# The two split instructions of each weight chunk, scheduled ahead of other ScalarE and VectorE work

## The chip, the core and the metric

The kernel runs on one core of a Trainium2 chip. The core has a matrix engine (TensorE, PE in the profile), three engines for elementwise work (VectorE, DVE; ScalarE, ACT; GpSimd, POOL), an engine that issues most DMA transfers (SyncE, SP), and an on-chip memory that its 16 DMA engines fill. Each engine runs its own list of instructions; semaphores make one wait for another. The metric is the device time of one execution in microseconds.

## What is computed

Two layers of an encoder over x of shape (1, 256, 2048), in float32:

```python
def even_layer(x, ...):
    proj = rmsnorm(x, norm_g) @ w_in              # 2048 x 6144: q, k, v, u, z_a, z_b
    o_a = chunked_relpos_attention(q, k, v, rel_bias) * silu(z_a)   # 16 heads x 64
    y = gelu(s5_ssm(u, ...))                      # 64 groups, complex state of 64
    o_b = y * sigmoid(y @ w_glu + b_glu) * silu(z_b)
    return x + concatenate([o_a, o_b]) @ w_out    # 2048 x 2048

def odd_layer(x, ...):
    proj = rmsnorm(x, norm_g) @ w_in              # q, k, v, z of 2048 columns, 16 forget logits
    o = forgetting_attention(q, k, v, log_sigmoid(f_logit + b_forget)) * silu(z)  # 16 heads x 128
    return x + o @ w_out
```

and a last rmsnorm. By far most of the work is the products with the weights: 256 rows times about 150 MB of float32 weights, each of which is used once.

## The kernel before

**Weights.** They are streamed in 296 chunks of 256 x 512 values (512 KB), in the order in which the products use them. TensorE computes a float32 product as three products of a shorter format, so that each chunk is split into a high part and a rest. `next_w` (line 116 on) does this for chunk i: SyncE loads it into wr_i (line 128, four buffers), ScalarE copies it into wh_i, rounded (line 131, three buffers), and VectorE writes the rest wl_i = wr_i - wh_i (line 132, three buffers). The last four chunks go into buffers lh and ll that stay.

**Products.** `project` takes the chunks of one 512-column tile, 8 of them for most products, and does 12 matmuls of 128 x 512 with each: for both halves of the 256 rows and both blocks of 128 rows of the chunk, high x wh (line 142), high x wl (line 143), low x wh (line 144). TensorE can begin a chunk when wh is there, needs wl for its second kind of matmul, and releases both buffers with the last.

**Stages.** Chunks 0 to 15 give u, the input of the S5 mixer; 16 to 23 z_b and 24 to 39 z_a, while VectorE and GpSimd compute the S5 tables beside them; 40 to 87 q, k and v in two halves, while VectorE runs the S5 scan (lines 428 to 431, 128 x 128 a step) and the attention of the head pairs a0/a1 to a14/a15; 88 to 95 the second half of z_b; 96 to 103 the GLU; 104 to 135 the output product. Between chunks 79 and 88 TensorE also computes the S5 outputs (py, lines 514 and 518) from tables T and mo, written to DRAM earlier and loaded by SyncE and GpSimd (lines 503 and 508). Layer 1 takes 32 chunks (q, k, v, z) for each of four groups of heads, 136 to 263, with the attention of heads c0 to c15 among them, and 264 to 295 for the output product.

**One head's softmax.** TensorE computes scores psc (lines 460 to 462), VectorE adds a bias and takes the row maximum (lg, mx, nm; lines 469 to 474), ScalarE takes the exponentials (lines 476 and 477), VectorE scales (rs, lg; lines 479 to 482), TensorE transposes into pp (line 485), VectorE copies to pT (line 487). VectorE and ScalarE do this between the splits of the chunks that TensorE works on meanwhile.

**What sets the order.** No order is written out by hand: the program is given in the order of its mathematics, and a scheduler places each instruction on its engine's list, with a simulated clock, the ready instruction of the highest priority first. Priority follows the order of the program. An engine then runs its list from first to last.

## Time and profile before

| | us |
|---|---|
| runs shown | 997.0, 997.74, 1001.69 |
| their median | 997.74 |
| span of the profiled execution | 995.2 |

The profile is of one execution: when each instruction began, how long it ran, and what ended the idle time before it. The span is the time from its first instruction to its last; the time of this execution as a run isn't on record, and the median of the runs lies 2.5 us above the span. Buffer numbers are left out in the profile (wl stands for all wl_i), so a single chunk is found by counting and by its time.

### The profile page before, as it was taken

What the parts mean: (1) busy time and instruction counts of PE and PEld (TensorE: products, weight loads), DVE (VectorE), ACT (ScalarE), POOL (GpSimd) and SP (SyncE); (2) the same over time, 40 slices, a digit from 0 to 9 for tenths busy, and PEclk for the clock granted to TensorE, in tenths of its full rate; (3) what the DMA queues carried; (4) which work ended last, traced back from release to release, by engine and by line L of the source; (5) the groups of instructions that cost most, each with busy time, mean ns of one, the idle gap of its engine ahead of it and who ended that gap; (6) DMA issues with size and microseconds to landing.
All of it is one profiled execution on the core that took longest, in us unless ns stands there. A gap on an engine that the chain in (4) does not pass through costs nothing.

```text
span 995.2 us, 13310 instructions
## 1 busy us (share of the span) xinstructions
PE 946.9 (95%) x4828; PEld 762.9 (77%) x4828; DVE 626.4 (63%) x1071; ACT 495.7 (50%) x717; POOL 184.6 (19%) x182
## 2 busy tenths in 40 slices
PE   7968788999999999999999999999999999999996
PEld 5856566887776777788888888888888888888874
DVE  7899999499962467855555445444544554455464
ACT  6623444454463367654444555445645554555451
POOL 2297974100003011000000321011001100100210
PEclk9987999999999999999999999999999999999998
DMA  8774655875569965566664654555455545554652
GB/s 303 281 218 147 189 165 175 241 214 178 163 204 263 266 207 179 167 200 204 204 225 149 212 195 153 190 182 191 155 191 184 170 153 191 185 170 155 194 196 90
DMA packets 72577, 191.47 MB, mean 192 GB/s; under 512 B 7488, under 2 KB 27184, under 8 KB 72128
## 3 DMA queue, kind: packets, MB, share of 16 engines
q1 hardware_dynamic: 71520, 188.93, 59.5%
q0 software_dynamic: 992, 1.69, 0.9%
q8 instruction: 38, 0.62, 0.3%
q14 instruction: 27, 0.22, 0.1%
HBM read 180.09 MB, written 10.50 MB: 192 GB/s over the span
## 4 chain that ended last, share of the span: by engine, by line
PE 74%; DVE 15%; DMA 4%; issue 4%; SPq 1%; ACT 1%; POOL 0%; POOLq 0%; DVEq 0%; ACTq 0%
DVE wl L132 5%; PE acc_oe L143 3%; PE acc_oe L142 3%; PE acc_oe L144 3%; PE acc_cv L142 3%; PE acc_cq L143 3%; PE acc_cq L144 3%; PE acc_cq L142 3%; PE acc_ck L142 3%; PE acc_cv L144 3%; PE acc_cv L143 3%; PE acc_cz L143 3%; PE acc_cz L144 3%; PE acc_cz L142 3%; PE acc_ck L144 3%
## 5 line engine op out<-in xcount | busy, mean ns | idle before, releaser
L132 DVE TENSOR_TENSOR wl<-wr,wh 128x1024 fp32r<-128x1024 f32 (+1 forms) x292 | 372.9, 1280 | 281.5 <-ACT wh L131 278.6
L131 ACT ACTIVATE wh<-wr 128x1024 fp32r<-128x1024 f32 (+1 forms) x292 | 307.6, 1056 | 338.8 <-PE acc_ck L144 41.8
L722 POOL TENSOR_SCALAR cbt<-ckb,cum 128x128 f32<-128x128 f32 x16 | 17.8, 1111 | 323.7 <-DVE mx_c L471 265.4
L143 PE MATMUL acc_cv<-wl,x1Th 128*128 128x512 f32 x128 | 51.1, 399 | 0.0
L143 PE MATMUL acc_oe<-wl,cTh 128*128 128x512 f32 x128 | 51.0, 399 | 0.0
L143 PE MATMUL acc_cq<-wl,x1Th 128*128 128x512 f32 x128 | 50.8, 397 | 0.0
L143 PE MATMUL acc_cz<-wl,x1Th 128*128 128x512 f32 x128 | 50.6, 395 | 0.0
L144 PE MATMUL acc_cq<-wh,x1Tl 128*128 128x512 f32 x128 | 50.5, 395 | 0.0
L144 PE MATMUL acc_oe<-wh,cTl 128*128 128x512 f32 x128 | 50.5, 395 | 0.0
L144 PE MATMUL acc_cv<-wh,x1Tl 128*128 128x512 f32 x128 | 50.3, 393 | 0.0
L144 PE MATMUL acc_cz<-wh,x1Tl 128*128 128x512 f32 x128 | 50.2, 392 | 0.0
L143 PE MATMUL acc_ck<-wl,x1Th 128*128 128x512 f32 x128 | 49.9, 390 | 0.0
L144 PE MATMUL acc_ck<-wh,x1Tl 128*128 128x512 f32 x128 | 49.9, 390 | 0.0
L142 PE MATMUL acc_cq<-wh,x1Th 128*128 128x512 f32 x128 | 48.7, 400 | 0.0
L142 PE MATMUL acc_cz<-wh,x1Th 128*128 128x512 f32 x128 | 47.6, 400 | 0.0
L142 PE MATMUL acc_oe<-wh,cTh 128*128 128x512 f32 x128 | 47.6, 399 | 0.0
L142 PE MATMUL acc_cv<-wh,x1Th 128*128 128x512 f32 x128 | 47.3, 398 | 0.0
L142 PE MATMUL acc_ck<-wh,x1Th 128*128 128x512 f32 x128 | 46.5, 392 | 0.0
L143 PE MATMUL acc_oo<-wl,oTh 128*128 128x512 f32 x108 | 42.5, 393 | 0.5 <-DVE wl L132 0.5
L144 PE MATMUL acc_oo<-wh,oTl 128*128 128x512 f32 x108 | 42.2, 391 | 0.0
L142 PE MATMUL acc_oo<-wh,oTh 128*128 128x512 f32 x108 | 39.7, 394 | 0.0
L143 PE MATMUL acc_zb<-wl,xTh 128*128 128x512 f32 x64 | 28.3, 442 | 9.4 <-DVE wl L132 9.4
(391 smaller groups left out, 2137.9 us busy)
## 6 DMA issues: line engine op xcount, KB each, us to landing
wr<-in_w_dram SPq DMA_DIRECT2D x295, 512.0 KB, 3.5
m_d<-mx SPq DMA_DIRECT2D x8, 512.0 KB, 4.9
mo<-m_d SPq DMA_DIRECT2D x8, 512.0 KB, 7.5
T<-k_d SPq DMA_DIRECT2D x40, 64.0 KB, 6.7
bc<-in_s5bc_dram SPq DMA_DIRECT2D x8, 256.0 KB, 3.3
xt<-in_x_dram SPq DMA_DIRECT2D x2, 1024.0 KB, 8.2
k_d<-ks SPq DMA_DIRECT2D x8, 256.0 KB, 3.4
bt<-in_rbx_dram SPq DMA_DIRECT2D x8, 256.0 KB, 3.7
```

The lines of the kernel that those rows point to most:

```text
L131: nc.scalar.activation(wh[:, c], raw[:, c], AF.Copy)
L132: nc.vector.tensor_tensor(wl[:, c], raw[:, c], wh[:, c].bitcast(F32), op=ALU.subtract)
L142: nc.tensor.matmul(acc[t], sh, wh[:, c], start=kb == 0, stop=False)
L143: nc.tensor.matmul(acc[t], sh, wl[:, c], start=False, stop=False)
L144: nc.tensor.matmul(acc[t], sl, wh[:, c], start=False, stop=kb == nkb - 1)
L722: W.tensor_scalar(bt[:, 0, :], ckb[:, hh, 0:P], cum[:, 0, h:h + 1], None, op0=ALU.add)
```

## The change

The two instructions of the split get a priority that is 3000 steps of the program earlier than their place. The DMA of line 128 is not in the block, and no other instruction is touched. Apart from this, the diff takes comments and docstrings out, not shown here; line numbers behind the new line are one or two higher.

```diff
@@
+SPLIT_AHEAD = 3000
@@ def next_w(split=None, dst=None):
             nc.sync.dma_start(raw[:, c], a["w"][i][:, c])
             if split:
                 split(o // NT)
-            nc.scalar.activation(wh[:, c], raw[:, c], AF.Copy)
-            nc.vector.tensor_tensor(wl[:, c], raw[:, c], wh[:, c].bitcast(F32), op=ALU.subtract)
+            with tc.high_priority(offset=SPLIT_AHEAD):
+                nc.scalar.activation(wh[:, c], raw[:, c], AF.Copy)
+                nc.vector.tensor_tensor(wl[:, c], raw[:, c], wh[:, c].bitcast(F32), op=ALU.subtract)
```

What the scheduler makes of it shows in the engines' lists. VectorE in the scan, around the split of chunk 57; st1, st2 and X are the four steps of the scan. Before:

```order
L430 TENSOR_TENSOR st2_1235<-st2_1235,X_806 128x128
L431 TENSOR_TENSOR X_806<-st1_1234,st2_1235 128x128
L132 TENSOR_TENSOR wl_57_2647<-wr_57_2645,wh_57_2646 128x1024
L428 TENSOR_TENSOR st2_1235<-e2_431,X_806 128x128
L429 TENSOR_TENSOR st1_1234<-e1t_434,X_806 128x128
L430 TENSOR_TENSOR st2_1235<-st2_1235,X_806 128x128
```

and now:

```order
L433 TENSOR_TENSOR X_806<-st1_1234,st2_1235 128x128
L430 TENSOR_TENSOR st2_1235<-e2_431,X_806 128x128
L431 TENSOR_TENSOR st1_1234<-e1t_434,X_806 128x128
L134 TENSOR_TENSOR wl_57_2647<-wr_57_2645,wh_57_2646 128x1024
L432 TENSOR_TENSOR st2_1235<-st2_1235,X_806 128x128
L433 TENSOR_TENSOR X_806<-st1_1234,st2_1235 128x128
```

The split stood behind a whole scan step and stands now between two of its rows, at a place one later in VectorE's list.

VectorE at the softmax of heads a4 and a5, around the splits of chunks 72 and 73. Before, from the negated maxima nm on; the eight rows of lg and mx come just ahead of these:

```order
L474 TENSOR_SCALAR nm_a4_2261<-mx_a4_2258 128x2
L474 TENSOR_SCALAR nm_a5_2280<-mx_a5_2277 128x2
L132 TENSOR_TENSOR wl_72_2963<-wr_72_2961,wh_72_2962 128x1024
L479 RECIPROCAL rs_a4_2266<-sm_a4_2263 128x2
L481 TENSOR_SCALAR lg_a4_2257<-lg_a4_2257,rs_a4_2266 128x128
L482 TENSOR_SCALAR lg_a4_2257<-lg_a4_2257,rs_a4_2266 128x256
L479 RECIPROCAL rs_a5_2285<-sm_a5_2282 128x2
L481 TENSOR_SCALAR lg_a5_2276<-lg_a5_2276,rs_a5_2285 128x128
L482 TENSOR_SCALAR lg_a5_2276<-lg_a5_2276,rs_a5_2285 128x256
L132 TENSOR_TENSOR wl_73_2981<-wr_73_2979,wh_73_2980 128x1024
```

and now:

```order
L134 TENSOR_TENSOR wl_72_2963<-wr_72_2961,wh_72_2962 128x1024
L134 TENSOR_TENSOR wl_73_2981<-wr_73_2979,wh_73_2980 128x1024
L471 ISA lg_a4_2257,mx_a4_2258<-psc_a4_2251,bt_0_2_2248 128x128
L471 ISA mx_a4_2258 128x1
L473 ISA lg_a4_2257,mx_a4_2258<-psc_a4_2251,bt_0_2_2248 128x256
L473 ISA mx_a4_2258 128x1
L471 ISA lg_a5_2276,mx_a5_2277<-psc_a5_2252,bt_0_2_2248 128x128
L471 ISA mx_a5_2277 128x1
L473 ISA lg_a5_2276,mx_a5_2277<-psc_a5_2252,bt_0_2_2248 128x256
L473 ISA mx_a5_2277 128x1
L476 TENSOR_SCALAR nm_a4_2261<-mx_a4_2258 128x2
L476 TENSOR_SCALAR nm_a5_2280<-mx_a5_2277 128x2
```

Both splits have moved ahead of the first softmax row of a4.

SyncE's queue at the S5 outputs; T and mo are the tables that TensorE multiplies with, wr the next weight chunks. Before:

```order
L128 DMA wr_84_3398<-in_w_dram 128x1024
L503 DMA T_4_2466<-k_d_193 16x8x128 x5
L508 DMA mo_4_2475<-m_d_194 128x1024
L503 DMA T_5_2495<-k_d_193 16x8x128 x5
L508 DMA mo_5_2504<-m_d_194 128x1024
L128 DMA wr_85_3416<-in_w_dram 128x1024
L128 DMA wr_86_3434<-in_w_dram 128x1024
L503 DMA T_6_2524<-k_d_193 16x8x128 x5
L508 DMA mo_6_2533<-m_d_194 128x1024
L503 DMA T_7_2553<-k_d_193 16x8x128 x5
L508 DMA mo_7_2562<-m_d_194 128x1024
L128 DMA wr_87_3452<-in_w_dram 128x1024
```

and now:

```order
L129 DMA wr_84_3398<-in_w_dram 128x1024
L505 DMA T_4_2466<-k_d_193 16x8x128 x5
L510 DMA mo_4_2475<-m_d_194 128x1024
L129 DMA wr_85_3416<-in_w_dram 128x1024
L505 DMA T_5_2495<-k_d_193 16x8x128 x5
L510 DMA mo_5_2504<-m_d_194 128x1024
L129 DMA wr_86_3434<-in_w_dram 128x1024
L129 DMA wr_87_3452<-in_w_dram 128x1024
L505 DMA T_6_2524<-k_d_193 16x8x128 x5
L510 DMA mo_6_2533<-m_d_194 128x1024
L505 DMA T_7_2553<-k_d_193 16x8x128 x5
L510 DMA mo_7_2562<-m_d_194 128x1024
```

The loads of chunks 85 and 87 are issued ahead of two and four of the loads of tables that they stood behind.

## Rows read from the trace of the kernel before

**Rows 1.** Which engines are busy: the page's part 1, the whole span.
```profile
PE 946.9 (95%) x4828; PEld 762.9 (77%) x4828; DVE 626.4 (63%) x1071; ACT 495.7 (50%) x717; POOL 184.6 (19%) x182
```

**Rows 2.** Table by stretches: start:end, length, busy us (instructions) of each engine, clock, DMA.
```profile
150.00:175.00 25.00, 21.47 (x153) 16.75 (x153) 24.73 (x28) 10.27 (x17) 10.73 (x7) 0.97 0.58 173
175.00:200.00 25.00, 25.00 (x163) 20.29 (x162) 9.89 (x15) 13.22 (x20) 3.97 (x9) 1.00 0.88 238
225.00:250.00 25.00, 23.27 (x104) 17.77 (x103) 24.52 (x64) 12.85 (x20) 0.20 (x1) 1.00 0.51 167
250.00:275.00 25.00, 23.94 (x117) 18.86 (x116) 24.73 (x65) 11.68 (x20) 0.33 (x1) 1.00 0.54 178
300.00:325.00 25.00, 22.72 (x201) 17.25 (x200) 7.35 (x6) 9.10 (x12) 6.92 (x14) 0.94 1.08 268
325.00:350.00 25.00, 24.05 (x187) 17.58 (x180) 10.80 (x15) 8.57 (x13) 1.57 (x3) 0.99 0.98 255
700.00:800.00 100.00, 100.00 (x478) 83.31 (x477) 48.39 (x74) 54.33 (x74) 11.14 (x19) 1.00 0.53 173
```

**Rows 3.** What TensorE waited for: us in total, times, longest us.
```profile
PE acc_za L143 <- DVE wl L132: 9.6, 5, 4.1
PE acc_zb L143 <- DVE wl L132: 9.4, 4, 5.7
...
PE py L518 <- DMA mo<-m_d: 2.5, 2, 1.9
PE acc_v L143 <- DVE wl L132: 1.6, 2, 1.2
...
PE acc_q L143 <- DVE wl L132: 1.1, 2, 0.8
```

**Rows 4.** The two splits, page's part 5: busy, mean ns, idle time before.
```profile
L132 DVE TENSOR_TENSOR wl<-wr,wh 128x1024 fp32r<-128x1024 f32 (+1 forms) x292 | 372.9, 1280 | 281.5 <-ACT wh L131 278.6
L131 ACT ACTIVATE wh<-wr 128x1024 fp32r<-128x1024 f32 (+1 forms) x292 | 307.6, 1056 | 338.8 <-PE acc_ck L144 41.8
```

**Rows 5.** Order of time, a stretch of stage 1: start, length in us.
```profile
59.48 2.25 POOL L358 TENSOR_TENSOR tm<-pi,cc 128x1152 f32<-128x1152 f32 x1 [0.69 <-DVE pi L287]
59.53 3.28 DVE L132 TENSOR_TENSOR wl<-wr,wh 128x1024 fp32r<-128x1024 f32 x1
```

**Rows 6.** Order of time, chunk 57 in the scan; idle time in brackets.
```profile
230.69 1.21 DVE L132 TENSOR_TENSOR wl<-wr,wh 128x1024 fp32r<-128x1024 f32 x1
...
231.96 0.50 PE L143 MATMUL acc_v<-wl,xTh 128*128 128x512 f32 x1 [1.19 <-DVE wl L132]
```

**Rows 7.** Order of time, softmax of a4 and a5, splits around it.
```profile
276.44 0.29 DVE L469 CUSTOM_DVE_ANT_0 lg_a<-psc_a,bt 128x128 f32<-128x128 f32 x1 [0.83 <-issue]
...
277.01 1.06 ACT L131 ACTIVATE wh<-wr 128x1024 fp32r<-128x1024 f32 x1 [2.72 <-PE acc_q L144]
...
280.31 0.35 DVE L482 TENSOR_SCALAR lg_a<-lg_a,rs_a 128x256 f32<-128x256 f32 x1
...
282.27 0.39 PE L142 MATMUL acc_k<-wh,xTh 128*128 128x512 f32 x1
...
282.50 0.39 PE L143 MATMUL acc_k<-wl,xTh 128*128 128x512 f32 x1
...
283.64 0.60 PE L485 MATMUL pp_a<-ident,lg_a 128*128 128x128 f32 x4
```

**Rows 8.** Order of time, TensorE, the S5 output steps.
```profile
320.93 0.43 PE L518 MATMUL py<-mo,X 128*32 128x128 f32 x8 [1.93 <-DMA mo<-m_d]
```

**Rows 9.** Order of time, softmax of a12 and a13.
```profile
385.39 0.28 DVE L469 CUSTOM_DVE_ANT_0 lg_a<-psc_a,bt 128x128 f32<-128x128 f32 x1
...
389.00 0.35 DVE L482 TENSOR_SCALAR lg_a<-lg_a,rs_a 128x256 f32<-128x256 f32 x1
```

**Rows 10.** Order of time, softmax of head c4 of layer 1.
```profile
663.45 0.17 DVE L479 RECIPROCAL rs_c<-sm_c 128x2 f32<-128x2 f32 x1 [1.05 <-ACT lg_c L477]
...
667.06 0.27 PE L485 MATMUL pp_c<-ident,lg_c 128*128 128x128 f32 x1
```

## The prediction

> **What bounds the kernel now.** I read the busy times first, then a table of the span by stretches, then the list of what TensorE waited for, and only then single instructions. TensorE is busy 95% of the 995.2 us span, VectorE 63%, ScalarE 50% [rows 1]. The table by stretches says where the missing 5% lies [rows 2]: from 350 us to 950 us TensorE has no idle time at all (one of these stretches is shown), so there a weight split that comes earlier can give nothing back. It is short of work in three places only: up to 175 us, where VectorE is full with the S5 tables (24.73 of 25 us busy in the last of these stretches); at 225 to 275 us, where VectorE is full again with the S5 scan; and at 300 to 350 us, where VectorE has time (7.35 of 25 us) and the DMA queues don't (1.08 and 0.98 of their share). The list of waits fits [rows 3]: TensorE waited for wl 9.6 us in the za projection, 9.4 in zb, 1.6 in v and 1.1 in q. These 21.7 us are all that an earlier wl could return. They belong to chunks 17 to 39 (the first two entries, stage 1) and 57 to 67 (the other two, the scan). The idle time in front of the splits themselves is the other way round: wh waits for TensorE, which has to release one of three buffers [rows 4]. In most of the kernel the splits are already as early as a buffer allows.

> **Stage 1, 0 to 200 us: nothing.** By the order of instructions, the change moves 190 of 1073 VectorE rows, 119 of 634 on ScalarE and 536 of 4425 on TensorE, but hardly any of them here. TensorE's rows are the same up to chunk 27. On VectorE three splits move by two or three rows: wl_10 and wl_26, for which TensorE did not wait anyhow, and wl_34, which passes three rows of the tables, about 1.7 us of work, on an engine that is full. What wl_34 gains is lost in front of wl_36, for the same rows still have to run; I take 0, with 1 us either way. The 19 us of waiting for chunks 17 to 39 stay, since in front of those chunks the order of VectorE's rows is what it was.

> [...] The trace shows a split that ran 3.28 us from 59.53 us, against a mean of 1.28 for all 292 [rows 4, 5]; a POOL operation had begun at 59.48 and ended at 61.73, and the split ended 1.1 us after that. [...]

> **The scan, 205 to 280 us: +0.4.** The 21.7 us have 2.7 here, and the idle time of the two stretches is 25 - 23.27 + 25 - 23.94 = 2.8 us [rows 2, 3]: that is the most that can be gained. But counted by the work ahead of them on VectorE, the splits move by -1.6 to +0.6 us only. wl_57, for which TensorE waited 1.19 us [rows 6], stands behind one more scan row than before, as the order shows, because rows of the softmax ahead of it have gone elsewhere and scan steps came forward. wl_62 and wl_65 come 1.3 and 1.6 us earlier. Against that the softmax of heads a0 to a3 comes 3.2 to 4.6 us later on VectorE, and TensorE's steps for it are 2.8 to 3.8 us later in its own order, so 0 to 1 us is to be paid there. Bounds: -2.8 (all idle time gone) and +1.2 (one split ahead of a softmax, its mean 1.28, rows 4). Taken: +0.4, near zero, as VectorE is full and the work is the same.

> **Heads a4 and a5, 276 to 290 us: +0.5.** Here the order changes as the change says: wl_72 and wl_73 now stand ahead of the first softmax row of a4. The split of chunk 73 needs wh_73, which waits for TensorE to end chunk 70, and the softmax rows wait behind it, because an engine takes its rows in order. Before, this chain ran from 276.44 to 280.66 us on VectorE, and TensorE came to pp_a at 283.64: 3.0 us of slack [rows 7]. In the new order TensorE has about 22 matmuls between the scores and pp_a4, at the 0.23 us from one to the next [rows 7] 5.0 us, and the chain of 4.2 us gets one wh (1.06) put into it, and one wl (1.28) ahead of its second head. 4.2 + 1.06 + 1.28 = 6.5 against 5.0 + 0.6 for pp_a4 itself + 0.9 for the matmuls in front of pp_a5 = 6.5. Just even: bounds 0 and 1.3, taken 0.5.

> **The T and mo loads, 300 to 350 us: +0.4.** The DMA of wr isn't raised, but its buffer comes free when the split is done, so it moves too. On SyncE's queue wr_85 passes from behind T_5 and mo_5 to ahead of them, and wr_87 passes T_6, mo_6, T_7 and mo_7. TensorE waits here for mo (2.5 us in all, 1.93 the longest) [rows 3, 8], and the two stretches are 2.28 + 0.95 = 3.2 us short of full [rows 2]. Bounds: -3.2, and for the loss the time that a chunk of 0.52 MB occupies the DMA engines at the 255 to 268 GB/s of these stretches, 2.0 us each, so +4.0. In TensorE's order the S5 output steps are later by 0.2 to 3.2 us too, which takes most of it up: +0.4.

> **Heads a12 and a13, 384 to 391 us: +0.6.** The chain took 389.35 - 385.39 = 4.0 us [rows 9], and TensorE had 28 matmuls between scores and pp_a12. In the new order it has 12: 12 x 0.23 + 0.9 for the scores = 3.6 us. A stall of 0.4 to 0.7, at most one wl more; the attention steps of the other pairs come out with slack.

> **Layer 1, 540 us on: +0.2.** The order moves splits ahead of parts of the softmax, about one chunk's worth of TensorE. For head c4 wl_189 and wl_190 now stand ahead of the second half of its row maximum. Its probabilities were ready at about 663.5, where 1/sum begins, and pp_c came at 667.06 [rows 10]: with a split (1.28) ahead 2.3 us stay. The weight chunks keep 2 to 3 us. Only c0, whose bias came late, is close: 0.2. From chunk 269 on the order is the same.

> Sum: 0 + 0.4 + 0.5 + 0.4 + 0.6 + 0.2 = +2.1 us. The profiled execution's span of 995.2 lies 2.5 below the median of the three runs, 997.74; I add the sum to the median: **999.8 us**. That is within 0.5% (992.75 to 1002.7), about what a measurement of this kernel can tell from no change.

> **Rivals.** (1) The waits for wl vanish: VectorE works them off first, the tables and the scan give way to 175 to 200 us, where VectorE is busy 9.89 of 25 us [rows 2]. All 21.7 us gone would be 976; two or three of the long ones, 9 us, 989. For it: the waits are real and there is room behind. Against it: the order in front of those chunks doesn't change. (2) Slower, by in-order engines: a raised split that waits for TensorE to release its buffer stands ahead of the exponentials and holds them up, and TensorE then waits at pp. The place is every head: 8 pairs in layer 0, 16 heads in layer 1. In the trace ScalarE stood 2.72 us before wh with only exponentials behind it [rows 7], and such waits for TensorE are the usual case [rows 4]. It decides where chain + 1.06 + 1.28 passes the TensorE work between scores and pp: 4.0 + 2.3 = 6.3 us against 5.0 to 6 in a few places of layer 0, 6 to 8 in most heads. At 0.5 us in each of 24 it is +12, 1010; in the 8 pairs alone and one load behind a weight, +4 + 2 = 1004. [...] (3) The change hardly does what it says, since raising an instruction that isn't ready moves nothing: then all terms are zero, 998, and the verdict is that of the forecast.

> **How the numbers follow.** The forecast with rival 3, no change that can be told: 0.68. Rival 2: 0.21, two thirds of it near 1004 to 1006, the rest up to 1012. Rival 1: 0.11, mostly its weak form or a better scan and better loads (-2.8 - 3.2 = -6.0: 992). The bounds of the unknown costs, added: -1 - 2.8 - 3.2 = -7 and 1 + 1.2 + 1.3 + 4 + 1.2 + 2 = +10.7; they don't come all at once, so the range is 992.5 to 1006. Faster 0.11, same 0.68, slower 0.21.

> **What would show it.** Right: the waits for wl in za and zb still near 19 us in all, TensorE again full from 400 to 950 us, stalls of half a microsecond at pp_a near 284 and 387, the stretch 300 to 350 us within 2 us of before. The forecast falls if the waits for wl in zb and za shrink by over 5 us (rival 1), or if waits of pp_a and pp_c for VectorE, which the list of waits doesn't have now, add up to over 5 us (rival 2).

## The result, and the profile after

The changed kernel takes 1006.02 us, the median of five runs (1004.03 to 1006.58), against 997.05 (994.79 to 1001.69) for the kernel before. The ratio is 1.0078, with a 95% interval of 1.0057 to 1.0100: slower by 0.6 to 1.0%. The forecast of 999.8 us, 2.1 more than before, and of no change that can be told did not hold; the median lies at the upper end of the range of 992.5 to 1006, where rival 2 stood. The profiled execution has a span of 1002.3 us, 7.1 more than before.

The page's first part hardly differs from [rows 1]; ScalarE is 4.5 us less busy, most of it because the new order needs three table loads fewer, of 1.28 us each. Run e2 below has the same three fewer and is no faster than before.

```profile
PE 948.4 (95%) x4828; PEld 762.4 (76%) x4828; DVE 628.3 (63%) x1071; ACT 491.2 (49%) x714; POOL 178.8 (18%) x182
```

What TensorE waited for (total, times, longest), to be held against [rows 3]:

```profile
PE acc_zb L145 <- DVE wl L134: 11.2, 3, 6.5
PE acc_za L145 <- DVE wl L134: 9.4, 7, 2.8
...
PE py L516 <- DMA T<-k_d: 2.4, 1, 2.4
PE acc_v L145 <- DVE wl L134: 2.1, 2, 1.6
PE py L520 <- DMA mo<-m_d: 2.1, 2, 1.1
PE acc_glu L144 <- DVE ob L611: 1.5, 1, 1.5
...
PE acc_q L145 <- DVE wl L134: 1.2, 2, 0.8
...
PE acc_k L144 <- ACT q L546: 0.3, 1, 0.3
...
PE pp_a L487 <- DVE lg_a L483: 0.3, 1, 0.3
```

The waits for wl in zb and za are 20.6 us, where they were 19.0: what the change is named for did not happen, as forecast. New in the list are T as well as mo for py, the GLU's accumulators waiting for VectorE (1.5), and two short ones (acc_k for ScalarE's copy of q, pp_a). The table by stretches, to be held against [rows 2]:

```profile
225.00:250.00 25.00, 22.72 (x100) 16.90 (x99) 24.48 (x61) 10.97 (x14) 0.00 (x0) 1.00 0.50 166
250.00:275.00 25.00, 23.84 (x117) 18.61 (x116) 24.49 (x65) 13.28 (x26) 0.40 (x2) 1.00 0.56 172
300.00:325.00 25.00, 23.34 (x215) 17.28 (x213) 8.02 (x7) 10.26 (x14) 7.93 (x16) 1.00 1.02 244
325.00:350.00 25.00, 21.80 (x173) 16.39 (x174) 7.58 (x9) 6.45 (x8) 1.68 (x4) 0.86 1.00 271
400.00:425.00 25.00, 23.75 (x126) 17.11 (x127) 20.23 (x45) 17.94 (x31) 0.00 (x0) 1.00 0.48 158
700.00:800.00 100.00, 100.00 (x480) 83.27 (x478) 49.53 (x73) 50.21 (x68) 10.08 (x17) 1.00 0.53 174
```

TensorE is again full in 700 to 800 us. It lost 0.6 us more at 225 to 250, and in 325 to 350 it is 3.2 us short of full at a granted clock of 0.86 (before: 0.95 short, at 0.99). In 400 to 425, where it had no idle time before, it is now short by 1.25 us.

To place the difference I gave each row of TensorE its usual time to the next (the median over both traces of rows that nothing held up) and counted by how much an execution is behind that sum when it has done the same amount of work. This frees the comparison from the new order of the rows. Places in TensorE's list are told below in the same usual times. The difference to the profile before, by stretches of before, in us:

| kernel | to 205 | 205-276 scan | 276-296 a4/a5 | 296-352 S5 outputs | 352-390 | 390-440 GLU | 440-960 |
|---|---|---|---|---|---|---|---|
| the change | -0.7 | +0.9 | +0.9 | +2.7 | +0.2 | +3.1 | +0.2 |
| e1_mid | +0.3 | +0.9 | 0.0 | +2.0 | +0.5 | +2.3 | 0.0 |
| e2_layer1 | +0.6 | 0.0 | 0.0 | +0.3 | 0.0 | 0.0 | +0.2 |
| e3_bias_buffer | -0.8 | +0.8 | +0.9 | +3.3 | +0.3 | +1.9 | +0.2 |
| e4_two_loads | +1.4 | +0.9 | +0.9 | +2.0 | +0.3 | +2.2 | +0.2 |
| e5_only_58 | 0.0 | +0.3 | +0.3 | +5.0 | +0.2 | +2.6 | 0.0 |
| e6_all_but_58 | +0.9 | +2.5 | -0.1 | -1.5 | 0.0 | 0.0 | +0.2 |
| e7_best | +1.1 | +2.5 | -0.1 | +0.2 | 0.0 | 0.0 | 0.0 |
| e8_extra_s5 | +2.6 | +0.1 | 0.0 | +3.3 | 0.0 | 0.0 | 0.0 |
| e9_extra_oe | +1.6 | 0.0 | 0.0 | +0.8 | 0.0 | 0.0 | 0.0 |

Each row is one profiled execution. The first column differs by 3 us among kernels that hardly differ or don't differ there (e8 and e9 have the order of before), so it says nothing; the S5 column of e2 and e9, where nothing was changed for the better or the worse, differs by 0.3 and 0.8. The other columns repeat well, but for the S5 column itself, which goes from 2.0 to 5.0 among the five kernels that have the change's order there. The loss of the change lies between 205 and 440 us, 7.8 us, and most of it in two places that are far from each other.

### The profile page after: what moved, and what is told of

It is laid out like the page before. It is cut to its first block, busy times and chain, and to the rows that moved or that the text cites. A ratio compares the mean times of both kernels' runs of the same rounds, so it can differ in the third digit from the quotient of the medians.

```text
span 1002.3 us, 13310 instructions
## 1 busy us (share of the span) xinstructions
PE 948.4 (95%) x4828; PEld 762.4 (76%) x4828; DVE 628.3 (63%) x1071; ACT 491.2 (49%) x714; POOL 178.8 (18%) x182
## 4 chain that ended last, share of the span: by engine, by line
PE 72%; DVE 17%; DMA 4%; issue 4%; ACT 1%; SPq 1%; POOL 0%; POOLq 0%; DVEq 0%; ACTq 0%
DVE wl L134 6%; PE acc_oe L145 3%; PE acc_oe L144 3%; PE acc_oe L146 3%; PE acc_cv L144 3%; PE acc_cq L145 3%; PE acc_cq L146 3%; PE acc_cq L144 3%; PE acc_ck L144 3%; PE acc_cv L145 3%; PE acc_cz L145 3%; PE acc_cz L146 3%; PE acc_cz L144 3%; PE acc_cv L146 3%; PE acc_ck L146 3%
## 5 line engine op out<-in xcount | busy, mean ns | idle before, releaser
L134 DVE TENSOR_TENSOR wl<-wr,wh 128x1024 fp32r<-128x1024 f32 (+1 forms) x292 | 366.7, 1258 | 300.9 <-ACT wh L133 298.8
L724 POOL TENSOR_SCALAR cbt<-ckb,cum 128x128 f32<-128x128 f32 x16 | 10.5, 654 | 328.6 <-DVE mx_c L473 270.9
```

The source lines that it names most:

```text
L134: nc.vector.tensor_tensor(wl[:, c], raw[:, c], wh[:, c].bitcast(F32), op=ALU.subtract)
L724: W.tensor_scalar(bt[:, 0, :], ckb[:, hh, 0:P], cum[:, 0, h:h + 1], None, op0=ALU.add)
```

## Where it starts

The chain could be followed back through both traces. ScalarE at the end of the k projection, before and after (start, length, engine, operation; the idle time in brackets); k is the copy of the two accumulators out of which the scores of heads a0 to a7 are made, qkT the copy of its transposes:

```profile
228.11 1.37 ACT L548 ACTIVATE k<-acc_k,rs 128x512 f32<-128x512 f32 x2 [0.97 <-PE acc_k L144]
229.38 1.05 ACT L131 ACTIVATE wh<-wr 128x1024 fp32r<-128x1024 f32 x1
234.91 1.06 ACT L131 ACTIVATE wh<-wr 128x1024 fp32r<-128x1024 f32 x1 [4.48 <-PE acc_v L144]
235.94 0.59 ACT L556 COPY qkT<-pqk 128x512 f32<-128x512 f32 x1
```

```profile
227.83 0.69 ACT L550 ACTIVATE k<-acc_k,rs 128x512 f32<-128x512 f32 x1 [1.42 <-PE acc_k L146]
228.53 1.06 ACT L133 ACTIVATE wh<-wr 128x1024 fp32r<-128x1024 f32 x1
229.49 0.67 ACT L550 ACTIVATE k<-acc_k,rs 128x512 f32<-128x512 f32 x1
234.94 1.06 ACT L133 ACTIVATE wh<-wr 128x1024 fp32r<-128x1024 f32 x1 [4.77 <-PE acc_v L146]
236.32 1.06 ACT L133 ACTIVATE wh<-wr 128x1024 fp32r<-128x1024 f32 x1 [0.32 <-PE acc_v L146]
237.28 0.57 ACT L558 COPY qkT<-pqk 128x512 f32<-128x512 f32 x1
```

Before, both halves of k ran as one piece (228.11, 1.37 us) and wh_58 after it. Now wh_58 stands between them, and further on wh_60, which waits for TensorE, stands ahead of qkT: qkT begins at 237.28 and not at 235.94. The first scores, psc of heads a0/a1, follow at 243.12 instead of 239.51 us; 2.7 us of this are product rows that now stand ahead of them in TensorE's list (TensorE, before and after):

```profile
239.51 0.49 PE L460 MATMUL psc_a<-qkT 64*128 64x128 f32 x4
```

```profile
243.12 0.49 PE L462 MATMUL psc_a<-qkT 64*128 64x128 f32 x4
```

From there each later step of the attention stands further back in TensorE's list, and so do the S5 outputs, whose first matmul comes at 298.94 and not at 295.93 us. T_2 can be loaded only when py_0 has released a buffer, so that its load is issued 3.0 us later (SyncE's queue, before and after):

```profile
296.85 2.22 SPq L503 DMA_DIRECT2D T<-k_d  x5
```

```profile
299.86 2.22 SPq L505 DMA_DIRECT2D T<-k_d  x5
```

Up to 306 us the DMA engines carry less for it: in the four stretches of 4 us from 290 us on their share is 0.05, 0.90, 0.74 and 0.87, where it was 0.40, 0.85, 0.97 and 1.09. From there to 342 us they are full in both kernels, 1.0 to 1.1 in all but one stretch.

The later start alone is not the loss. py_4, the first output that waits for these loads, also stands 1.3 us later in TensorE's list, and TensorE waits there for 1.4 us, where it waited for 2.3 before. The loss of this execution shows at py_5, for which TensorE had no wait before (TensorE, after):

```profile
327.21 0.43 PE L516 MATMUL py<-T,uT 128*32 128x128 f32 x8 [2.43 <-DMA T<-k_d]
328.63 0.66 PE L520 MATMUL py<-mo,X 128*32 128x128 f32 x8 [0.99 <-DMA mo<-m_d]
```

T_5 goes into a buffer that py_3 frees. py_3 stands 3.6 us later in TensorE's list and py_5 only 1.6. GpSimd issues its part of T_5 right after py_3, 4.8 us later than before. SyncE, where wr_85 now stands ahead of T_5, issues its own part another 3.2 us later; its list of waits has 3.4 us there for the landing of a weight load (before; after):

```profile
310.85 1.57 POOL L503 DMA_DIRECT2D T<-k_d  x3 [0.57 <-PE py L518]
```

```profile
315.61 1.57 POOL L505 DMA_DIRECT2D T<-k_d  x3 [3.52 <-PE py L520]
318.82 2.41 SPq L505 DMA_DIRECT2D T<-k_d  x5
```

So two things delay T_5: a later py_3, and the weight loads on SyncE's queue. How the waiting divides between py_4 and py_5 differs from run to run, but the sum of the two keeps apart: it is 4.9 us in the change and 4.2 to 5.6 in e1, e3 and e5 below, whose S5 outputs have the same order, against 2.3 before and 2.0 to 3.7 in e2 and e6 to e9 (e4 waits elsewhere). Which of the two things weighs more, the runs do not tell.

## The experiments

**Which splits matter: e1 and e2.** Only part of the chunks is raised, 40 to 69, and 136 on:

```diff
-            with tc.high_priority(offset=SPLIT_AHEAD):
+            with tc.high_priority(offset=SPLIT_AHEAD if 40 <= i < 70 else 0):   # e2: i >= 136
```

> Only the splits of chunks 40 to 69 (the scan) are raised; up to layer 1 the lists are then those of the change, and in layer 1 those of before. Theory A (the loss sits in three places between 205 and 425 us, S5 output loads about 3, GLU bias about 2, scan and heads a4/a5 about 1.5): slower by 6.5 to 8 us, as the whole change. Theory B (the softmax of many heads is held up behind raised splits, each a little, layer 1 too): 3 to 5 us, since the 16 heads of layer 1 are left as they were.

> Only the splits of chunks 136 on (layer 1) are raised. Theory A: within 1 us of before. Theory B: 3 us or more slower, with waits of pp_c for VectorE in the list.

e1: ratio 1.0058 (1.0036 to 1.0080), 5.8 us slower, 0.7 short of what theory A expected and 0.8 above theory B; the interval reaches into both. It has the same two large columns in the table as the change. e2: 1.0007 (0.9997 to 1.0018). The 16 heads of layer 1 cost nothing that can be told, and no pp_c is in its list of waits; for these heads theory B falls. Since e1's lists equal those of the change up to layer 1 but for a few rows, the loss in 296 to 440 us does not come from the splits that are raised there. That of a4/a5 does go with them: 0.0 in e1 against 0.9.

**The GLU bias: e3.** In the GLU, VectorE adds a bias bg to the accumulators. The bias is loaded into a buffer that the bias table bt of heads a12/a13 leaves free. In the change the scores of a12/a13 come at 393.9 instead of 383.5 us, the bias lands at 400.5, VectorE waits for it, and TensorE for the accumulators (after):

```profile
400.50 1.29 DVE L611 TENSOR_TENSOR ob<-acc_glu,bg 128x512 f32<-128x512 f32 x2 [1.10 <-DMA bg<-in_bglu_dram]
...
401.25 0.50 PE L144 MATMUL acc_glu<-wh,yTh 128*128 128x512 f32 x1 [1.47 <-DVE ob L611]
```

```diff
-        bg = at.tile([P, NT], F32, name=f"bg_{n}", tag="bt")
+        bg = wp.tile([P, NT], F32, name=f"bg_{n}", tag="sq", bufs=2)
```

> The whole change, but the GLU bias gets a buffer of its own kind (that of the later squares), so that its load no longer waits for the softmax of heads a12 and a13. Theory A: the wait of acc_glu for ob (1.47 us) goes, 1.5 to 2.2 us faster than the whole change, some 5 to 6 slower than before. Theory B: as the whole change, 7 to 8 slower than before, the wait only gets another name.

Measured: 1.0057 (1.0036 to 1.0079), 2.1 us less than the change's 1.0078, as theory A expected; but the intervals overlap, so that the times alone don't show it. The profile is clearer: the column of the GLU falls from 3.1 to 1.9, and of the wait 0.3 is left.

```profile
PE acc_glu L144 <- DVE ob L611: 0.3, 1, 0.3
```

In e1, e4 and e5, whose GLU has the order of the change, the wait is 0.7, 0.7 and 1.1, so the 1.5 of the change is at the high end. The bias load is worth about 0.4 to 1.2 us. Without this wait 1.5 to 1.6 of the column is left in all five, and it has no single cause: 0.3 and 0.4 us are lost ahead of pp_a12 and pp_a13, and a little at the changes between the product's matmuls and those of other shapes, where the step to the next row is up to 0.33 us instead of 0.23 and of which the new order has 29 in this column against 22.

**The queue of the weight loads: e4.** The prediction had put its term for the S5 outputs on wr_85 and wr_87, which pass T_5 to T_7 on SyncE's queue. Here POOL issues them:

```diff
-            nc.sync.dma_start(raw[:, c], a["w"][i][:, c])
+            (nc.gpsimd if i in (85, 87) else nc.sync).dma_start(raw[:, c], a["w"][i][:, c])
```

> The whole change, but the loads of chunks 85 and 87 are issued from POOL and not from SyncE; no row of TensorE, VectorE or ScalarE moves. Theory A with the queue as its cause (weight loads ahead of T_5 to T_7 on SyncE): the S5 outputs lose 0 to 1 us against before, not 3.2, and the whole is 2 to 3 us faster than the change. Rival C (TensorE's own order, with py_3 four us later so that the buffer of T_5 comes free later): no difference from the change, within 1 us.

Measured: 1.0073 (1.0051 to 1.0094), no better than the change; in the S5 column 2.0 against 2.7. Its waits:

```profile
PE py L516 <- issue: 4.2, 1, 4.2
...
PE py L520 <- DMA mo<-m_d: 0.7, 1, 0.7
PE acc_glu L144 <- DVE ob L611: 0.7, 1, 0.7
```

Theory A had expected 2 to 3 us less than the change; by its time the run is what rival C expected. The 2.4 us for T_5 at 327 us are gone, but 4.2 us stand at py_2 now, ahead of both loads that were moved, where POOL's part of the loads of T_2 had waited for a bias table that landed late; TensorE then came to py_5 later. Nor did the edit take the two weight loads out of the way: POOL issues wr_85 at 319.03 and wr_87 at 328.49, and the loads of T_5 and T_6 begin at 324.09 and 330.31. So e4 shows that a better place in SyncE's queue alone brings nothing that can be told. It does not show what the same weight loads cost ahead of the tables on the DMA engines.

**One split, and all but one: e5, e6, e7.** If the chain begins at wh_58, the split of this one chunk, wh_58 and wl_58, should do all of it:

```diff
-            with tc.high_priority(offset=SPLIT_AHEAD):
+            with tc.high_priority(offset=SPLIT_AHEAD if i == 58 else 0):        # e5
+            with tc.high_priority(offset=SPLIT_AHEAD if i != 58 else 0):        # e6
+            with tc.high_priority(offset=SPLIT_AHEAD if i < 136 and i != 58 else 0):   # e7
```

> Only the split of chunk 58 is raised, one of 292. On ScalarE this puts its wh between the two halves of the copy that takes k of the first head pairs out of the accumulators; the scores of heads a0/a1 then stand 2.8 us later in TensorE's list, and from there to the GLU the list is nearly that of the change. Theory D (the loss of the change starts at this one row and is passed on through the scores, the start of the S5 outputs and a DMA-bound stretch, and the GLU bias): 4.5 to 7 us slower than before, with py_0 some 3 us later and the stretch from there to 352 us of before longer by 2 to 3. Theory B (many small delays of the softmax by its own splits): within 1 us of before.

> The whole change without chunk 58. The scores of a0/a1 stand where they stood before, and py_0 1.1 us earlier in TensorE's list than before. Theory D: the loss goes, -2 to +1 us against before. Theory B: 5 to 8 slower, as the whole change, since 291 of 292 splits are still raised.

> As the run without chunk 58, and layer 1 (chunks 136 on) not raised either. Theory D: -2.5 to +0.5 us against before, at most 1 us away from the other. It is the version with most to gain, as S5 outputs begin earlier and layer 1 has nothing to win. Theory B: 3 to 5 slower.

e5, one chunk of 296: 1.0051 (1.0035 to 1.0068), 5.1 us slower, as theory D expected, with the S5 outputs and the GLU as its two places. The first column of the two, 5.0, is more than the 2 to 3 us that were expected there:

```profile
PE py L520 <- DMA mo<-m_d: 5.1, 3, 2.0
...
PE py L516 <- DMA T<-k_d: 2.5, 1, 2.5
...
PE acc_glu L144 <- DVE ob L611: 1.1, 1, 1.1
```

e6, the other 295: 1.0005 (0.9993 to 1.0017), no difference to before. This is the clearest result of the study: most of the loss of the change starts at the split of chunk 58, and theory B falls. How it is passed on through the S5 outputs the two runs do not settle, since everything goes together in them: in e5 wr_85 and wr_87 stand ahead of T_5 and T_6 in SyncE's queue as in the change, and in e6 and e7 they stand where they stood before. e6 has no column of the GLU and gains 1.5 us in the S5 outputs. It is not faster than before because it loses 2.5 us in the scan:

```profile
PE acc_za L145 <- DVE wl L134: 9.9, 6, 3.9
...
PE pp_a L487 <- DVE lg_a L483: 2.0, 2, 1.5
PE acc_v L145 <- DVE wl L134: 1.6, 1, 1.6
```

pp_a waits 2.0 us for VectorE there (heads a2/a3, up to 268 and 269 us). This comes near to rival 2, at one pair of heads, but it isn't its mechanism: one raised split stands just ahead of this softmax on VectorE, while between its rows stand steps of the scan, and pp_a stands 2.7 us earlier in TensorE's list than before. e7 was meant as the best version, with -2.5 to +0.5 us expected; at 1.0017 (1.0003 to 1.0031) it is 1.7 us slower than before. No version that beats the kernel before came out of the runs.

**Is 296 to 352 us bound by the DMA engines? e8 and e9.** The kernel before, with two weight chunks loaded twice into the same buffer, in that stretch (e8) and in the output product (e9). No row moves on TensorE, VectorE or ScalarE.

```diff
             nc.sync.dma_start(raw[:, c], a["w"][i][:, c])
+            if i in (84, 86):            # e9: (114, 116)
+                nc.sync.dma_start(raw[:, c], a["w"][i][:, c])
```

> The kernel before, with the weight chunks 84 and 86 loaded twice (0.52 MB each, once more into the same buffer); no row of TensorE, VectorE or ScalarE moves. The first extra load stands between mo_5 and T_6 on SyncE's queue, the second behind mo_7. If the stretch from 300 to 345 us is bound by what the DMA engines carry (theory D), each costs 2.0 us at 260 GB/s: 2 to 4 us slower. If only the order and the start of single loads matter there: 0 to 1 us.

> The same with chunks 114 and 116, in the output product of layer 0 (430 to 450 us), where TensorE has no idle time. Both theories: 0 to 0.5 us; it says what an extra load costs where the DMA engines have room.

e8: 1.0030 (1.0018 to 1.0042), 3.0 us slower, all of it in the S5 column. e9: 0.9995 (0.9985 to 1.0005). The same megabyte costs nothing in the output product, where the DMA engines carried 0.45 and 0.78 of their share before (430 to 440 and 440 to 450 us), and 3 us in the stretch where they are full (1.03 in 316 to 346 us, before and in e8). But e8's profile does not put most of this down to the sum of what is loaded. The second load of chunk 86 is issued behind mo_7; wh_86 waits for it, yn, the activation of the S5 outputs, stands behind wh_86 on ScalarE, and TensorE waits 1.9 us for yn (e8, ScalarE and TensorE):

```profile
341.83 1.06 ACT L133 ACTIVATE wh<-wr 128x1024 fp32r<-128x1024 f32 x1 [9.00 <-DMA wr<-in_w_dram]
...
343.21 0.65 PE L587 MATMUL poa<-pT_a,v 128*64 128x256 f32 x4 [1.85 <-ACT yn L522]
```

The waits of py are 4.2 us in all in e8, against 3.2 before, and they are 4.2 in e9 too, which loads nothing more in this stretch. So it is not shown that the stretch is bound by the sum of what the DMA engines carry, as theory D had it; it is shown that a chunk whose load comes late there is waited for.

## Where the prediction held and where it failed, point by point

- **No gain from wl, and the order in stage 1:** right. The 19 us of waits stayed (20.6), since the rows in front of those chunks are the same. Rival 1 was rightly small. The list of before has 1.3 us more of waits for wl than the 21.7 us that the prediction counted, 0.8 in u and 0.5 in the last product; it changes nothing.
- **Scan, +0.4:** measured +0.9. wl_57, which stands one scan row later, cost 1.6 instead of [rows 6]'s 1.19, and wl_59 a new 0.6. The direction was right.
- **a4 and a5, +0.5:** measured +0.9, but not where it was worked out: pp of a4 and a5 is not held up at all. 0.4 is lost where TensorE needs wl_74, whose wh stands between the exponentials, and 0.5 behind an accumulator that ScalarE freed late. The size came near by luck.
- **T and mo loads, +0.4: the step that failed.** Measured +2.7. Two things were in view, weight loads that pass the table loads, and S5 output steps that stand 0.2 to 3.2 us later in TensorE's order, and the prediction let the second make up for most of the first. It does so only where the step that needs a table has moved back as far as the step that frees its buffer. py_3, which frees T_5's buffer, moved by 3.6 us and py_5 by 1.6; T_5 went out 4.8 us later, on SyncE behind wr_85, and TensorE waited 3.4 us for T_5 and mo_5, where it had not waited before. How much of this belongs to the buffer and how much to wr_85 stays open. The upper bound of +4.0 was wide enough, the value taken from it was not.
- **a12 and a13, +0.6:** 0.3 and 0.4 lost ahead of their pp, as worked out. **Not seen at all:** the bias of the GLU, in a buffer that this softmax frees, 0.4 to 1.2 us, and further small gaps up to a column of 3.1. The prediction had looked at who reads the softmax, not at who gets its buffers.
- **Layer 1, +0.2:** measured +0.2, and e2 cannot be told from before.
- **Rival 2** had the right sign and a cause of the right kind, work on ScalarE held up by a raised split, but the wrong place and price: not 0.5 us in each of 24 heads, but the split of one chunk, and a price that is paid some 90 and 170 us later. By its own measure, waits of pp_a and pp_c, it would not have been found in the change: these are 0.3 us in all.

Three things stay open. What the 2.7 us of the S5 outputs are made of, the later start, the later buffers, wr_85 and wr_87 or the clock (below), no run takes apart. The part of the GLU column that is left without the bias wait, 1.6 us, was not taken apart by runs either. And why the first scores come 3.6 us later (243.12 against 239.51) when k is finished 0.7 us later (230.16 against 229.48) and the copy qkT begins 1.3 us later was not taken apart: e5 shows that the one split does it, not by which of the rows that were laid out anew behind it.

## What to carry to other kernels

Raising instructions does not only move them; it moves what they pass, and the whole order behind it is laid out anew. So look at the one or two rows on each engine that were passed and feed other stages (here a copy out of the accumulators), and follow them to the next load or buffer that hangs on them, far behind if need be. Where TensorE waits for loads, ask of each load which step frees its buffer and what stands ahead of it in its queue, and compare how far the step that frees the buffer has moved with how far the step that needs the load has moved: here 3.6 us against 1.6. And an experiment that adds or moves a load also moves the rows that wait for that load; look in its profile at what TensorE waited for before its time is put down to one cause.

## What the chip showed that was not expected

```profile
324.00:328.00 4.00, 1.21 (x12) 0.49 (x10) 0.00 (x0) 0.00 (x0) 1.11 (x3) 1.00 1.08 300
328.00:332.00 4.00, 3.37 (x29) 2.56 (x30) 0.00 (x0) 1.06 (x2) 1.57 (x3) 0.50 1.06 217
332.00:336.00 4.00, 4.00 (x13) 3.22 (x12) 1.23 (x1) 0.62 (x2) 0.00 (x0) 0.65 1.11 217
```

Only 13 matmuls ran in the last of these full 4 us: from 331.09 to 334.50 us those of the product stand 0.43 us apart, and from 335.10 us, at a clock of 1.00, 0.23. Before, the clock was 0.76 and 0.81 there, with a shorter gap:

```profile
320.00:324.00 4.00, 3.07 (x40) 2.06 (x44) 0.65 (x1) 1.44 (x2) 1.57 (x3) 0.76 1.02 337
324.00:328.00 4.00, 4.00 (x39) 3.11 (x32) 0.57 (x1) 0.63 (x2) 1.57 (x3) 0.81 1.13 231
```

Missing clock makes (0.50 + 0.35) x 4 = 3.4 us in the one and (0.24 + 0.19) x 4 = 1.7 us in the other. By this estimate, which counts the missing clock as lost time, up to 1.7 us of the 2.7 us of this stretch are clock and not waiting.
